# Block sums ordered between bank emptyings, and a weight sum made from another, in a two-layer hybrid attention trunk

## The chip, the cores and the metric

The kernel runs on one core of a Trainium2 chip. The core has five engines with instruction streams of their own: PE (matrix products), DVE (elementwise and reductions), ACT (pointwise functions and copies), POOL (elementwise on SBUF only) and SP (here it only issues DMAs). Each engine takes its instructions in the order in which the compiler put them, and one that waits holds up those behind it. The metric is the device time of one execution in microseconds (us), lower is better.

## The reference

A batch of one, 1024 tokens, width 1024, two layers, all in float32:

```python
for l in range(DEPTH):
    h = rmsnorm(x, norm1[l])
    proj = h @ w_in[l]
    qa, ka, va, qb, kb, vb, gate_pre = jnp.split(proj, splits, axis=-1)
    o_a = dilated_mixture(...)            # 12 heads in 3 groups of (window, dilation)
    o_b = stick_breaking_attention(...)   # 4 heads
    gates = jax.nn.sigmoid(gate_pre + b_gate[l])
    merged = g_a * (o_a @ w_br[l, :OUT_A]) + g_b * (o_b @ w_br[l, OUT_A:])
    x = x + merged @ w_o[l]
    up = rmsnorm(x, norm2[l]) @ w_up[l]
    a = causal_depthwise_conv(up[..., :D_FF], conv_w[l], conv_b[l])
    x = x + (jax.nn.gelu(a, approximate=False) * up[..., D_FF:]) @ w_down[l]
return rmsnorm(x, norm_f)
```

## The kernel before, in words

**Products.** Activations lie with features on the partitions and tokens in two halves of 512 columns. A float32 product is made of three matmuls: each operand is split into a high and a low part of a shorter type (ACT casts the high part, DVE subtracts it to get the low one; `split`, lines 138 and 145), and high x high, high x low and low x high are summed in a PSUM bank. "Emptying" a bank means reading it with ACT and DVE so that it can be used again; the tag "ps" has two banks.

**Seven products for eight.** Two 512-row halves of the contraction, two column blocks and two token halves form a 2 x 2 block product, done with seven block products instead of eight (a scheme of Strassen's kind). It needs sums of blocks on both sides. On the side of the weights `pair` (line 1055 on) makes them for each pair of column blocks: a raw tile `in_a` of four blocks a11, a12, a21, a22 is loaded, and its sums are formed on POOL (lines 1078 and 1080) and DVE (1084 and 1089), then split (`piece`) into the weights w1 to w7. On the side of the activations `block_sums` (line 1005 on) forms, once per layer and for each of four feature chunks i, from the blocks b11, b12, b21, b22 of h: sum 1 = b12 - b11, sum 3 = b22 - b12, sum 2 = b11 + sum 3 (DVE lines 1020, 1016, 1023) and sum 4 = b21 - sum 2 (POOL line 1026), and splits them (`in_two`) into S[1] to S[4]. `seven` (line 999 to 1001) issues the matmuls of one block product: 12 of them, in two steps of six.

**The stages of a layer.** First the *head*: queries, keys and values of the first two stick-breaking heads are made the plain way (`values_part`, banks v_ps, emptied on lines 576 and 577; `kq_half`, banks kq_ps and q_ps, emptied on lines 592 to 596). The block sums are issued beside it. Then the *attention*: 16 stick-breaking items (B), 4 near items (N) and 16 dilated items (T). Between their small steps the class `Dense` puts steps of the remaining projections, 18 pairs per layer, as filler: after each small step of an item, `advance(rate)` adds `rate` to what is due and runs one step (six matmuls) for each whole one. The rates are RATE by query block for B, RATE_N for N and RATE_T for T. Then come the branch projections, w_o, and the feed-forward part, which has blocks of its own and which the change doesn't touch.

**What sets the order.** PE's order is the order of the program text. The other engines' order is made by the compiler's list scheduler, in which what is emitted earlier goes first when it can; `tc.add_manual_dep(..., NO_SYNC)` adds an edge that keeps one instruction behind another in that order without a wait, SYNC one with a wait. `LAST["head"]` names the last two emptyings (ACT, DVE) of the head emitted so far, `LAST["h"]` the last instruction that makes h. A list `todo` in `block_sums` holds the small jobs; while the head runs, one job is popped after each step of the head (`dense.aside()`). `dense.prime(1)` runs one preparing step of the first pair. A pair prepares itself in six such steps (READY): load, first POOL sum or sums, w1, then w5 with the DVE sum for w6, then w6, then the DVE sum for w3. Later pairs take these steps while the pair before them runs.

**Buffers.** The raw tile `in_a` has two buffers ("ql"), the result tile `u` of a pair two ("wr", 1024 columns: halves u1 and u2). POOL writes the weight sum a11 - a21 into u2 of the new `u` (line 1078), and from there w7 is split; later u2 holds results.

**Only in the first layer**: h of the first 384 tokens is put together again from its two parts by POOL (`again`, line 1971 on, instruction 1977), eight instructions, into RAW[0, 0] (b12) and RAW[0, 1] (b22), alternating between them.

Of the kernel before, what the change touches and what calls it, by code (L numbers as in the profile page):

```python
# [7 lines left out]
F32 = mybir.dt.float32  # L8
# [4 lines left out]
ALU = mybir.AluOpType  # L13
# [3 lines left out]
P = 128  # L17
T = 1024
D = 1024
KD = D // P  # L20
HF = 512
# [11 lines left out]
NRAW = 2  # L33
# [5 lines left out]
SYNC = mybir.DependencyInfo(mybir.DependencyClass.Sync, mybir.DependencyReason.DATA)  # L39
NO_SYNC = mybir.DependencyInfo(mybir.DependencyClass.NoSync, mybir.DependencyReason.DATA)  # L40
IN_ORDER = {ET.PE, ET.Activation, ET.DVE, ET.Pool}
HEAD = 4
SECOND = 0.35
RATE = (1.1, 1.25, 1.35, 1.4)
RATE_N = 0.75
RATE_T = 0.55
EARLY = 5
LEAD = 6
LEAD_N = 7
# [7 lines left out]
def f32(ap):  # L57
    return ap.bitcast(F32)
# [3 lines left out]
def trunk_kernel(ctx, tc, x, norm1, w_in, b_gate, w_br, w_o, norm2, w_up, conv_w, conv_b, w_down, norm_f, out, depth=None, probe=None):  # L62
    nc = tc.nc
    act, dve, pe, pool = nc.scalar, nc.vector, nc.tensor, nc.gpsimd
# [4 lines left out]
    sb = ctx.enter_context(tc.tile_pool(name="sb", bufs=1))  # L69
# [15 lines left out]
    LAST = {}  # L85
# [39 lines left out]
    def small(name, dtype=F32):  # L125
        return sb.tile([P, 512], dtype, tag="pt", bufs=PT, name=name)
# [8 lines left out]
    def split(hi, lo, src, turn=None, behind=None):  # L135


        one = act.copy(hi, src)  # L138
        if behind:
            tc.add_manual_dep(one.ins, behind[0], NO_SYNC, reason="behind")  # L140
        if turn == "is":
            LAST["act"] = one.ins.name
        elif turn == "waits" and "act" in LAST:
            tc.add_manual_dep(one.ins, LAST["act"], NO_SYNC, reason="in turn")
        two = dve.tensor_tensor(lo, src, f32(hi), ALU.subtract)  # L145
        if behind:
            tc.add_manual_dep(two.ins, behind[1], NO_SYNC, reason="behind")
        if turn == "is":
            LAST["dve"] = two.ins.name
        return two  # L150
# [285 lines left out]
    H = [[None, None], [None, None]]  # L436
# [51 lines left out]
    S, B = {}, {}  # L488
# [15 lines left out]
    RAW = {}  # L504
# [479 lines left out]
    def yields(one):  # L984

        for k in ("red", "dve"):
            if k in LAST:
                tc.add_manual_dep(one.ins, LAST[k], NO_SYNC, reason="in turn")

    def piece(src, turn=None):  # L990
        hi = sb.tile([P, 512], F32R, tag="wh", bufs=4, name="w_hi")
        lo = sb.tile([P, 512], F32R, tag="wl", bufs=4, name="w_lo")
        yields(split(hi, lo, src, turn))
        return hi, lo
# [10 lines left out]
    def block_sums(dense):  # L1005


        b12, b22, b11, b21 = (lambda i, n=n, k=k: RAW[n, k][:, i, :] for n in range(2) for k in range(2))

        s3 = {}  # L1010

        def sum3(i):
            if i % 2 == 0:
                s3[i] = sb.tile([P, 2, HF], F32, tag="p4", bufs=4, name="h_sum")
                s3[i], s3[i + 1] = s3[i][:, 0, :], s3[i][:, 1, :]
            one = dve.tensor_tensor(s3[i], b22(i), b12(i), ALU.subtract)
            tc.add_manual_dep(one.ins, LAST["h"], NO_SYNC, reason="behind h")

        def sum1(i):
            dve.tensor_tensor(b12(i), b12(i), b11(i), ALU.subtract)  # L1020

        def sum2(i):
            dve.tensor_tensor(b11(i), b11(i), s3[i], ALU.add)

        def sum4(i):
            pool.tensor_tensor(b21(i), b21(i), b11(i), ALU.subtract)

        def in_two(t, i):
            if i == 0:
                if t == 4:  # L1030
                    S[4] = half(0, 0)
                else:
                    new_s(t)
            split(*S[t][i], {1: b12, 2: b11, 3: s3.get, 4: b21}[t](i), "waits", LAST["head"] if t > 2 else None)

        def front(i):
            sum3(i)
            sum1(i)
            in_two(1, i)
            sum2(i)  # L1040

        todo = [(set(), lambda i=i: front(i)) for i in range(4)]
        todo += [(set(), lambda: dense.prime(1)), (set(), lambda: [sum4(i) for i in range(4)])]
        todo += [({"wv"}, lambda: dense.prime(1))]
        todo += [(set(), lambda i=i: in_two(2, i)) for i in range(4)]
        todo += [(set(), lambda: dense.prime(1)) for _ in range(2)]

        def begin():
            for i in range(4):
                dense.at(1 + i, lambda i=i: in_two(3, i))  # L1050
                dense.at(6 + i, lambda i=i: in_two(4, i))

        return todo, begin

    def pair(dense, l, offs, tiled, put):

        def view(x, n=None):  # L1060

            return x.rearrange("p (r j) -> p r j", r=4) if tiled else x

        def grid(o):
            return o.rearrange("p (j r) -> p r j", r=4) if tiled else o

        raw = sb.tile([P, 4, 512], F32, tag="ql", bufs=2, name="in_a")
        for c in range(2):
            one = nc.sync.dma_start(
                raw[:, 2 * c : 2 * c + 2, :].rearrange("p a (k n) -> p (a k) n", n=P),  # L1070
                w_in[l][:, offs[c] : offs[c] + P].rearrange("(k p) n -> p k n", p=P),
            )
            tc.add_manual_dep(one.ins, LAST["sv"], NO_SYNC, reason="behind")
        a11, a12, a21, a22 = (raw[:, i, :] for i in range(4))
        yield
        u = sb.tile([P, T], F32, tag="wr", bufs=NRAW, name="u")
        u1, u2 = u[:, HF:T], u[:, 0:HF]
        one = pool.tensor_tensor(u2, a11, a21, ALU.subtract)  # L1078
        tc.add_manual_dep(one.ins, LAST["again"], NO_SYNC, reason="behind")
        pool.tensor_tensor(a21, a21, a22, ALU.add)  # L1080
        yield
        w1 = piece(a11)
        yield
        yields(dve.tensor_tensor(a11, a21, a11, ALU.subtract))
        w5 = piece(a21, "waits")
        yield
        w6 = piece(a11)
        yield
        yields(dve.tensor_tensor(a11, a12, a11, ALU.subtract))
        yield  # L1090
        w3 = piece(a11, "waits")
        u5 = small("u5")
        pa, pc = bank("ps", "i_a"), bank("ps", "i_c")
        yield from seven(pa, w1, half(1, 0), True, True)
        yield
        with tc.high_priority(offset=AHEAD):
            act.copy(view(u1), grid(pa))
        w7 = piece(u2, "waits")
        yield from seven(pc, w5, S[1], True, True)
        yield  # L1100
        with tc.high_priority(offset=AHEAD):
            act.copy(view(u5), grid(pc))
        w2 = piece(a12)
        yield from seven(pa, w6, S[2], False, True)
        with tc.high_priority(offset=AHEAD):
            act.copy(view(u2), grid(pa))
        w4 = piece(a22)
        dense.last(0)
        yield
        yield "turn"  # L1110
        yield from seven(pc, w3, half(0, 1), False, True)
        with tc.high_priority(offset=AHEAD):
            dve.tensor_tensor(view(u2), view(u2), grid(pc), ALU.add)
        put(0, 0, u2, False, a11)
        yield
        yield "turn"
        yield from seven(pa, w7, S[3], False, True)
        with tc.high_priority(offset=AHEAD):
            dve.tensor_tensor(view(u5), view(u5), grid(pa), ALU.add)
        put(1, 0, u5, False, a21)  # L1120
        dense.last(1)
        yield
        yield "turn"
        pb = bank("ps", "i_b")
        yield from seven(pb, w2, half(1, 1), True, True)
        with tc.high_priority(offset=AHEAD):
            dve.tensor_tensor(view(u1), view(u1), grid(pb), ALU.add)
        put(0, 1, u1, False, a12)
        yield
        yield "turn"  # L1130
        for word in seven(pa, w4, S[4], False, True):
            yield
            yield "turn"
        with tc.high_priority(offset=AHEAD):
            put(1, 1, grid(pa), True)
        yield
# [83 lines left out]
    def mixer(l, pending):  # L1220
# [44 lines left out]
        for j in range(16):  # L1265
            items.append((f"B{j}", [f"FB{j // 4 * 4 + 3}"], [], RATE[3 - j % 4], lambda j=j: stick_item(dense, j // 4, 3 - j % 4)))
        for v in range(4):
# [616 lines left out]
    def first():  # L1884
# [7 lines left out]
        wv = early["wv"] = []  # L1892
# [78 lines left out]
        def again():  # L1971

            t = slice(0, 3 * P)
            for e in range(KD):
                k = e % 2
                hi, lo = (f32(y[:, 4 * k + e // 2, t]) for y in H[0])
                one = pool.tensor_tensor(RAW[0, k][:, e // 2, t], hi, lo, ALU.add)
                tc.add_manual_dep(one.ins, LAST["h"], NO_SYNC if e else SYNC, reason="after h")
            LAST["again"] = one.ins.name

        def fill(n):
# [19 lines left out]
        f = [scaled(i) for i in range(8)]  # L2001
# [92 lines left out]
```

## Time and profile before

| what | value |
|---|---|
| device time, median of 3 runs | 2668.99 us (2664.97 to 2672.4) |
| device time of the profiled execution | 2669.75 us |
| its span, first to last instruction | 2667.6 us |
| mean granted clock of PE | 0.994 |
| busy PE / DVE / ACT / POOL, us | 2619.4 / 2072.7 / 1347.4 / 696.2 |
| head of layer 0, until its first pair | up to 77.17 us |
| head of layer 1, until its first pair | up to 1390.75 us |

The device time of the profiled execution is 2.15 us above its span. A row of a timeline reads: start in us, duration in us, engine (with q: its queue), line, operation, written tile <- read tiles, shapes, how many in a row, and in brackets how long the engine was idle before it and what ended that. A row of the waits reads: who waited for whom: us in total, times, the longest. A row of the windows reads: stretch, its length, busy time of PE, PE's weight loads, DVE, ACT and POOL with the number of instructions, PE's granted clock (1.00 is full), the share of the DMA engines and GB/s. A row of the groups ends in: busy us, mean ns of one | idle us before them.

### The profile page before, as it was taken

The numbers are of one execution on the slowest core, as the hardware profiler recorded it, in microseconds if no ns is written. First come the engines' busy times: TensorE is split into PE (matmuls) and PEld (weight loads), VectorE is DVE, ScalarE is ACT, GpSimd is POOL, SyncE is SP. The second block draws the span as 40 slices with busy tenths as digits, with TensorE's granted clock in tenths as the row PEclk, the third lists the DMA queues.
The fourth block names the chain that finished last, engine by engine and source line by source line (L and its number), as shares of the span: only waits on it lengthen the run. The fifth ranks groups of instructions, "written<-read, shape, count | busy, mean of one in ns | idle before, by whom it ended". The sixth has DMA issues, their size and how long they took to land.

```text
span 2667.6 us, 36682 instructions
## 1 busy us (share of the span) xinstructions
PE 2619.4 (98%) x12732; PEld 2190.2 (82%) x12732; DVE 2072.7 (78%) x3110; ACT 1347.4 (51%) x2500; POOL 696.2 (26%) x588
## 2 busy tenths in 40 slices
PE   8999999999999999999999999999999999999999
PEld 7887888888888888888888877888888888888887
DVE  7876767685888988897678777667858888898865
ACT  5545566564555554532445555666645455554225
POOL 4222110122233443321123112111321343344200
PEclk9999999999999999999999999999999999999999
DMA  6543487883244544688444344787732544446863
GB/s 226 154 123 107 144 216 204 201 262 107 83 139 146 171 137 156 227 317 318 151 131 147 121 133 140 207 226 194 233 99 71 175 141 151 150 168 248 339 243 116
DMA packets 400422, 468.26 MB, mean 176 GB/s; under 512 B 24308, under 2 KB 315500, under 8 KB 398444
## 3 DMA queue, kind: packets, MB, share of 16 engines
q1 hardware_dynamic: 400220, 465.90, 54.3%
q8 instruction: 101, 1.65, 0.3%
q14 instruction: 85, 0.70, 0.1%
q10 hardware_dynamic: 16, 0.00, 0.0%
HBM read 303.23 MB, written 162.59 MB: 175 GB/s over the span
## 4 chain that ended last, share of the span: by engine, by line
PE 84%; DVE 9%; DMA 3%; ACT 2%; issue 2%; POOL 0%; SPq 0%; DVEq 0%; ACTq 0%; POOLq 0%
PE u_a L999 5%; PE u_a L1000 5%; PE u_a L1001 5%; PE d_ps L1708 5%; PE d_ps L1710 4%; PE d_ps L1709 4%; PE i_a L999 4%; PE i_a L1001 4%; PE i_a L1000 4%; PE u_c L999 3%; PE u_c L1000 3%; PE u_c L1001 3%; PE o_ps L181 2%; PE o_ps L179 2%; PE o_ps L180 2%; PE i_c L999 2%
## 5 line engine op out<-in xcount | busy, mean ns | idle before, releaser
L145 DVE TENSOR_TENSOR w_lo<-up_a,w_hi 128x512 fp32r<-128x512 f32 x240 | 237.4, 996 | 21.7 <-ACT w_hi L138 21.7
L138 ACT CAST w_hi<-up_a 128x512 fp32r<-128x512 f32 x240 | 149.3, 622 | 185.4 <-PE u_a L1000 45.4
L138 ACT CAST w_hi<-in_a 128x512 fp32r<-128x512 f32 x216 | 134.1, 621 | 185.3 <-PE i_a L1000 71.3
L1716 DVE TENSOR_TENSOR x<-x,d_ps 128x512 f32<-128x512 f32 (+1 forms) x228 | 152.0, 671 | 77.9 <-PE d_ps L1710 76.7
L145 DVE TENSOR_TENSOR w_lo<-in_a,w_hi 128x512 fp32r<-128x512 f32 x216 | 161.4, 748 | 51.7 <-ACT w_hi L138 43.7
L1447 POOL TENSOR_TENSOR cv<-cv 128x512 f32<-128x512 f32 x88 | 132.3, 1515 | 249.6 <-DVE cv L1442 139.4
L1078 POOL TENSOR_TENSOR u<-in_a 128x512 f32<-128x512 f32 x36 | 52.6, 1460 | 399.9 <-DMA in_a<-in_w_in_dram 118.0
L145 DVE TENSOR_TENSOR g<-cv,g 128x512 fp32r<-128x512 f32 x154 | 152.2, 990 | 5.2 <-ACT g L138 2.7
L1708 PE MATMUL d_ps<-gd_in,w_hi 128*128 128x512 f32 (+1 forms) x340 | 130.3, 383 | 1.5 <-ACT w_hi L138 0.7
L1710 PE MATMUL d_ps<-gd_in,w_lo 128*128 128x512 f32 (+1 forms) x340 | 129.8, 382 | 0.0
L1709 PE MATMUL d_ps<-gd_in,w_hi 128*128 128x512 f32 (+1 forms) x340 | 129.8, 382 | 0.0
L999 PE MATMUL u_a<-hh,w_hi 128*128 128x512 f32 x320 | 124.7, 390 | 2.0 <-DVE u L1598 2.0
L1001 PE MATMUL u_a<-t_hi,w_lo 128*128 128x512 f32 x320 | 124.5, 389 | 0.0
L1000 PE MATMUL u_a<-hl,w_hi 128*128 128x512 f32 x320 | 124.5, 389 | 0.0
L1000 PE MATMUL u_a<-t_lo,w_hi 128*128 128x512 f32 x320 | 124.5, 389 | 0.0
L1001 PE MATMUL u_a<-hh,w_lo 128*128 128x512 f32 x320 | 124.5, 389 | 0.0
L999 PE MATMUL u_a<-t_hi,w_hi 128*128 128x512 f32 x320 | 124.5, 389 | 0.0
L720 DVE TENSOR_TENSOR_SCAN stay<-stay,zero 128x512 f32<-128x512 f32 (+2 forms) x96 | 97.2, 1020 | 33.2 <-POOL stay L707 33.0
L999 PE MATMUL i_a<-t_hi,w_hi 128*128 128x512 f32 x288 | 119.9, 416 | 0.0
L999 PE MATMUL i_a<-hh,w_hi 128*128 128x512 f32 x288 | 119.2, 414 | 0.0
L138 ACT CAST g<-cv 128x512 fp32r<-128x512 f32 x154 | 95.0, 617 | 41.4 <-POOL cv L1447 29.9
L1001 PE MATMUL i_a<-t_hi,w_lo 128*128 128x512 f32 x288 | 114.5, 398 | 0.0
(384 smaller groups left out, 8443.4 us busy)
## 6 DMA issues: line engine op xcount, KB each, us to landing
gd<-g SPq DMA_DIRECT2D x154, 512.0 KB, 3.5
gd_in<-gd SPq DMA_DIRECT2D x154, 512.0 KB, 5.7
up_a<-in_w_up_dram SPq DMA_DIRECT2D x80, 512.0 KB, 5.3
in_a<-in_w_in_dram SPq DMA_DIRECT2D x72, 512.0 KB, 5.6
wd_raw<-in_w_down_dram SPq DMA_DIRECT2D x22, 1024.0 KB, 11.4
gin<-gs SPq DMA_DIRECT2D x32, 512.0 KB, 4.6
w_raw<-in_w_o_dram SPq DMA_DIRECT2D x64, 256.0 KB, 2.8
gs<-u SPq DMA_DIRECT2D x48, 256.0 KB, 3.6
```

The lines of the kernel that those rows point to most:

```text
L138: one = act.copy(hi, src)
L145: two = dve.tensor_tensor(lo, src, f32(hi), ALU.subtract)
L179: pe.matmul(o, lh, rh, start=(first and i == 0), stop=False, skip_group_check=share)
L720: one = dve.tensor_tensor_scan(rev, rev, zero[:, 0:1].to_broadcast([P, c1 - c0]), 1.0 if c1 == L else sv[:, c1 : c1 + 1], ALU.mult, ALU.add)
L999: pe.matmul(o, w[0][:, c], rh, start=(first and i == 0), stop=False, skip_group_check=True)
L1000: pe.matmul(o, w[0][:, c], rl, start=False, stop=False, skip_group_check=True)
L1001: pe.matmul(o, w[1][:, c], rh, start=False, stop=(last and i == 3), skip_group_check=True)
L1447: return lambda: pool.tensor_tensor(dst, a, b, ALU.subtract)
L1708: pe.matmul(o[:, sub], wh[:, c], gh[:, sub], start=(i == 0 and k in (0, 4, 5)), stop=False, skip_group_check=True)
L1709: pe.matmul(o[:, sub], wh[:, c], gl[:, sub], start=False, stop=False, skip_group_check=True)
L1710: pe.matmul(o[:, sub], wl[:, c], gh[:, sub], start=False, stop=(i == m - 1), skip_group_check=True)
L1716: dve.tensor_tensor(x, x, o[:, sub], ALU.add)
```

## The change

Four things are changed.

1. In `block_sums` sum 1 comes first for all four chunks and is written to a new tile (`free`, tag "p4") instead of over b12; sum 3 and sum 2 come later, together, as `sum32`. Every one of them is now put behind the emptying of the head that was emitted last (`behind`), and so are all splits (`in_two`; before: those of S[3] and S[4] only). The list of jobs is rewritten: sum 1 and S[1] in the first four jobs, then sum 3 with sum 2 chunk by chunk, sum 4, and S[2] in two jobs with an empty one between.
2. In `pair` the POOL sum a11 - a21 is gone. In its place POOL makes a22 - w6 (the same value, as w6 = a21 + a22 - a11), into a21, in the sixth preparing step, just ahead of the DVE sum for w3 that overwrites w6. The tile `u` is taken after the preparing steps, and w7 is split from a21.
3. The filler rates of the stick-breaking items fall by 0.05 each, that of the dilated ones rises from 0.55 to 0.62.
4. In `again` the order follows b12, then b22, and each of the eight instructions is synchronised with the last part of h emitted by then (before: the first only).

```diff
-RATE = (1.1, 1.25, 1.35, 1.4)
+RATE = (1.05, 1.2, 1.3, 1.35)
...
-RATE_T = 0.55
+RATE_T = 0.62
...
+        def behind(one, eng=1):
+            tc.add_manual_dep(one.ins, LAST["head"][eng], NO_SYNC, reason="behind")
 
         def sum1(i):
-            dve.tensor_tensor(b12(i), b12(i), b11(i), ALU.subtract)
-
-        def sum2(i):
-            dve.tensor_tensor(b11(i), b11(i), s3[i], ALU.add)
+            one = dve.tensor_tensor(free(1, i), b12(i), b11(i), ALU.subtract)
+            behind(one)
+            tc.add_manual_dep(one.ins, LAST["h"], NO_SYNC, reason="behind")
+
+        def sum32(i):
+            behind(dve.tensor_tensor(free(3, i), b22(i), b12(i), ALU.subtract))
+            behind(dve.tensor_tensor(b11(i), b11(i), room[3, i], ALU.add))
...
-        def front(i):
-            sum3(i)
-            sum1(i)
-            in_two(1, i)
-            sum2(i)
-
-        todo = [(set(), lambda i=i: front(i)) for i in range(4)]
-        todo += [(set(), lambda: dense.prime(1)), (set(), lambda: [sum4(i) for i in range(4)])]
-        todo += [({"wv"}, lambda: dense.prime(1))]
-        todo += [(set(), lambda i=i: in_two(2, i)) for i in range(4)]
-        todo += [(set(), lambda: dense.prime(1)) for _ in range(2)]
...
+        todo = [
+            do(*each(sum1, (0,), (1,))),
+            do(*each(sum1, (2,), (3,))),
+            do(*each(in_two, (1, 0), (1, 1))),
+            do(*each(in_two, (1, 2), (1, 3))),
+            do(prime),
+            do(*each(sum32, (0,))),
+            do(*each(sum32, (1,))),
+            do(*each(sum32, (2,))),
+            nothing,
+            do(*each(sum32, (3,)), *each(sum4, (0,), (1,), (2,), (3,))),
+            ({"wv"}, prime),
+            do(*each(in_two, (2, 0), (2, 1))),
+            nothing,
+            do(*each(in_two, (2, 2), (2, 3))),
+            do(prime),
+            do(prime),
+        ]
...
         yield
-        u = sb.tile([P, T], F32, tag="wr", bufs=NRAW, name="u")
-        u1, u2 = u[:, HF:T], u[:, 0:HF]
-        one = pool.tensor_tensor(u2, a11, a21, ALU.subtract)
+        one = pool.tensor_tensor(a21, a21, a22, ALU.add)
         tc.add_manual_dep(one.ins, LAST["again"], NO_SYNC, reason="behind")
-        pool.tensor_tensor(a21, a21, a22, ALU.add)
         yield
         w1 = piece(a11)
...
+        pool.tensor_tensor(a21, a22, a11, ALU.subtract)
         yields(dve.tensor_tensor(a11, a12, a11, ALU.subtract))
         yield
         w3 = piece(a11, "waits")
+        u = sb.tile([P, T], F32, tag="wr", bufs=NRAW, name="u")
+        u1, u2 = u[:, HF:T], u[:, 0:HF]
         u5 = small("u5")
...
-        w7 = piece(u2, "waits")
+        w7 = piece(a21, "waits")
...
             for e in range(KD):
-                k = e % 2
-                hi, lo = (f32(y[:, 4 * k + e // 2, t]) for y in H[0])
-                one = pool.tensor_tensor(RAW[0, k][:, e // 2, t], hi, lo, ALU.add)
-                tc.add_manual_dep(one.ins, LAST["h"], NO_SYNC if e else SYNC, reason="after h")
+                hi, lo = (f32(y[:, e, t]) for y in H[0])
+                one = pool.tensor_tensor(RAW[0, e // 4][:, e % 4, t], hi, lo, ALU.add)
+                tc.add_manual_dep(one.ins, LAST["h"], SYNC, reason="after h")
```

More of the change, by code (lines that the diff above doesn't have):

```diff
@@ L1008, in block_sums, with free @@
         b12, b22, b11, b21 = (lambda i, n=n, k=k: RAW[n, k][:, i, :] for n in range(2) for k in range(2))
-        s3 = {}
-        def sum3(i):
+        room = {}
+        def free(t, i):
             if i % 2 == 0:
[L1014 to L1017, printed above, removed]
-        def sum1(i):
-            dve.tensor_tensor(b12(i), b12(i), b11(i), ALU.subtract)
-        def sum2(i):
-            dve.tensor_tensor(b11(i), b11(i), s3[i], ALU.add)
+                x = sb.tile([P, 2, HF], F32, tag="p4", bufs=4, name="h_sum")
+                room[t, i], room[t, i + 1] = x[:, 0, :], x[:, 1, :]
+            return room[t, i]
+        def behind(one, eng=1):
+            tc.add_manual_dep(one.ins, LAST["head"][eng], NO_SYNC, reason="behind")
+        def sum1(i):
+            one = dve.tensor_tensor(free(1, i), b12(i), b11(i), ALU.subtract)
[4 more added lines that the diff above has]
+            behind(dve.tensor_tensor(b11(i), b11(i), room[3, i], ALU.add))
         def sum4(i):
@@ L1033, in in_two, with do, each @@
                     new_s(t)
-            split(*S[t][i], {1: b12, 2: b11, 3: s3.get, 4: b21}[t](i), "waits", LAST["head"] if t > 2 else None)
-        def front(i):
-            sum3(i)
-            sum1(i)
-            in_two(1, i)
-            sum2(i)
-        todo = [(set(), lambda i=i: front(i)) for i in range(4)]
-        todo += [(set(), lambda: dense.prime(1)), (set(), lambda: [sum4(i) for i in range(4)])]
-        todo += [({"wv"}, lambda: dense.prime(1))]
-        todo += [(set(), lambda i=i: in_two(2, i)) for i in range(4)]
-        todo += [(set(), lambda: dense.prime(1)) for _ in range(2)]
+            src = room[t, i] if t in (1, 3) else (b11 if t == 2 else b21)(i)
+            split(*S[t][i], src, "waits", LAST["head"])
+        def do(*fs):
+            return set(), lambda: [f() for f in fs]
+        def each(f, *args):
+            return [lambda x=x: f(*x) for x in args]
+        nothing = (set(), lambda: None)
+        prime = lambda: dense.prime(1)
+        todo = [
[16 more added lines that the diff above has]
+        ]
         def begin():
```

## The prediction, made before the changed kernel was run

> **What bounds the kernel now.** The page comes first, for the engine that is nearly always busy.
>
> ```profile
> span 2667.6 us, 36682 instructions
> PE 2619.4 (98%) x12732; PEld 2190.2 (82%) x12732; DVE 2072.7 (78%) x3110; ACT 1347.4 (51%) x2500; POOL 696.2 (26%) x588
> ```
>
> PE is the bound, and the change neither adds nor removes a matmul. What can be won is 48.2 us in which PE is idle, and what its clock loses behind such waits. So the waits of PE are next, the longest first.
>
> ```profile
> PE kq_ps L179 <- DVE vb L577: 9.3, 1, 9.3
> PE sb_o L745 <- DVE vv L1181: 5.9, 2, 2.9
> PE q_ps L179 <- DVE kq_l L593: 4.3, 1, 4.3
> PE sb_t L732 <- DVE beta L724: 3.6, 2, 1.9
> PE z L636 <- DMA t_kq<-tk: 2.9, 3, 1.6
> ```
>
> These five rows are 26.0 us in nine waits. The first lies in the head of layer 0, the third in that of layer 1; sb_o and sb_t belong to stick-breaking items, z <- t_kq to dilated ones. The windows around them show what the clock adds.
>
> ```profile
> 50.00:75.00 25.00, 15.73 (x80) 13.52 (x80) 21.33 (x26) 8.27 (x15) 8.85 (x6) 0.80 0.35 115
> 250.00:275.00 25.00, 22.07 (x101) 18.05 (x100) 12.72 (x21) 11.18 (x23) 4.66 (x7) 0.86 0.31 106
> 625.00:650.00 25.00, 25.00 (x112) 20.68 (x111) 10.61 (x16) 9.50 (x16) 5.10 (x4) 1.00 0.37 107
> 1350.00:1375.00 25.00, 20.66 (x88) 16.85 (x88) 24.84 (x29) 9.39 (x18) 16.67 (x11) 0.93 0.53 163
> 1550.00:1575.00 25.00, 22.08 (x119) 18.45 (x118) 16.72 (x27) 10.84 (x20) 4.14 (x6) 1.00 0.34 105
> ```
>
> At full clock an undisturbed stretch issues 112 large matmuls in 25 us, 0.223 us each; a filler step of six is 1.34 us. The wait at 257 is followed by a lowered clock (0.86), the equally long one at 1571 is not (1.00).
>
> **The change part by part. The head of layer 0.** DVE's timeline shows what stands ahead of the emptying that PE waits for, and PE's what the wait leaves behind.
>
> ```profile
> 47.19 2.10 DVE L1016 TENSOR_TENSOR h_sum<-h_raw 128x512 f32<-128x512 f32 x2
> 62.47 0.68 DVE L1023 TENSOR_TENSOR h_raw<-h_raw,h_sum 128x512 f32<-128x512 f32 x1
> 63.07 1.27 DVE L577 TENSOR_TENSOR vb<-v_ps,vb 128x512 fp32r<-128x512 f32 x2
> 64.97 2.48 DVE L145 TENSOR_TENSOR t_lo<-h_raw,t_hi 128x512 fp32r<-128x512 f32 x4
> 71.81 0.69 DVE L596 TENSOR_TENSOR kq_l<-kq_ps,kq_h 128x512 fp32r<-128x512 f32 x1 [1.64 <-ACT kq_h L595]
> 72.42 0.68 DVE L145 TENSOR_TENSOR w_lo<-in_a,w_hi 128x512 fp32r<-128x512 f32 x1
> ```
> ```profile
> 63.80 0.80 PE L179 MATMUL kq_ps<-hh,kq_w 128*128 128x512 f32 x1 [9.27 <-DVE vb L577]
> 67.31 0.40 PE L181 MATMUL kq_ps<-hh,kq_w 128*128 128x512 f32 x1
> 70.99 0.39 PE L179 MATMUL q_ps<-hh,kq_w 128*128 128x512 f32 x1
> 76.20 0.39 PE L181 MATMUL q_ps<-hh,kq_w 128*128 128x512 f32 x1
> 77.17 0.50 PE L999 MATMUL i_a<-hh,w_hi 128*128 128x512 f32 x1
> ```
>
> PE has the values in their two banks at 63.80 - 9.27 = 54.53. From 47.19 on DVE works through four chunks of four instructions (sum 3, sum 1, low part of S[1], sum 2), 16 in the 15.88 us until 63.07, 0.99 each, and only then empties the two banks. After the wait PE is slow: from 63.80 to 67.31 lie 8 intervals, 3.51 us, where the 23 intervals from 70.99 to 76.20 take 0.2265 each, so 1.81; the price is 1.70. Wait and clock cost 10.97.
>
> After the change only eight of the 16 are emitted ahead of the first emptying (four sums 1, four low parts); sums 3 and 2 are kept behind it. At the same 0.99 these end at 47.19 + 7.9 = 55.1, the emptying (1.27 / 2 = 0.64) at 55.8. PE waits 1.3 instead of 9.27. Then keys run for 24 x 0.2265 = 5.4 until 61.2, while DVE has six sums (5.9 at 0.99, 3.7 at the 0.62 of the quiet row x4) and the second emptying: done between 60.1 and 62.3, so at most 1.1 is left, of which I take 0.5. **Gain: 10.97 - 1.3 - 0.5 = 9.2.** Bounds: 10.97 if both leftovers vanish; 2.4 in the first rival below.
>
> What is late next: the first pair, which starts at 77.17 now and at 68 then. S[1] is done by 55, and the first preparing steps stand at the same places of the head. S[2] is needed two products (24 matmuls, 5.4 us) after the start, at 73.4. In DVE's queue 29 instructions stand from 47.19 to the end of the row at 72.42 (73.10), with that row's 1.64 idle and a little more among them: 24 us of work, which, started at 47.19, ends at 71. It is enough, with 2 us to spare. The loads of the stick items' keys and of the second pair are issued behind the same emptyings and move with them.
>
> **`again`.** Three of its eight POOL instructions ran early, beside DVE; now all eight run late.
>
> ```profile
> 33.43 2.94 POOL L1977 TENSOR_TENSOR h_raw<-hh,hl 128x384 f32<-128x384 f32 x3
> 35.41 1.52 DVE L145 TENSOR_TENSOR hl<-h_raw,hh 128x512 fp32r<-128x512 f32 x1 [0.21 <-ACT hh L138]
> 42.34 5.81 POOL L1977 TENSOR_TENSOR h_raw<-hh,hl 128x384 f32<-128x384 f32 x5 [5.96 <-DVE hl L145]
> ```
>
> The DVE row beside them takes 1.52 where a quiet one takes 0.62; it may win 0.9. The eight then end at 42.34 + 8 x 1.16 = 51.6, with b12 complete at 47.0, in time for sum 1. Beside the sums DVE may lose what the three took, up to 2.9. I take 0 of -0.9 to +2.9.
>
> **The head of layer 1.** Here the emptying of the queries stands behind the sums.
>
> ```profile
> 1358.09 0.68 DVE L596 TENSOR_TENSOR kq_l<-kq_ps,kq_h 128x512 fp32r<-128x512 f32 x1
> 1358.69 1.78 DVE L1016 TENSOR_TENSOR h_sum<-h_raw 128x512 f32<-128x512 f32 x2
> 1370.77 0.68 DVE L593 SCALAR_TENSOR_TENSOR kq_l<-q_ps,kq_h 128x512 fp32r<-128x512 f32 x1
> 1371.50 0.80 PE L179 MATMUL q_ps<-hh,kq_w 128*128 128x512 f32 x1 [4.34 <-DVE kq_l L593]
> ```
>
> PE finished the matmuls before at 1367.16. Twelve sums fill the 12.1 us from 1358.69 to 1370.77. Four of them, or eight with the low parts, are ahead of the queries' emptying after the change: 4 to 8 us at 1.0, done at 1363.4 to 1367.4, about when PE comes. The wait of 4.34 goes, and with it the low clock (0.93), for which I take layer 0's 1.70. **Gain: 6.0**, between 4 and 6.
>
> **The pair's sums, and u late.** One of the two waits of sb_o:
>
> ```profile
> 252.19 1.77 POOL L1078 TENSOR_TENSOR u<-in_a 128x512 f32<-128x512 f32 x1 [5.89 <-PE v_t L1175]
> 253.09 0.59 ACT L704 ACTIVATE stay<-z 128x512 f32<-128x512 f32 x1
> 255.53 0.30 POOL L707 TENSOR_SCALAR_AFFINE_SELECT stay<-stay 128x128 f32<-128x128 f32 x1
> 255.86 1.23 DVE L720 TENSOR_TENSOR_SCAN stay<-stay,zero 128x512 f32<-128x512 f32 x1 [3.05 <-POOL stay L707]
> 259.15 0.55 PE L745 MATMUL sb_o<-sbh,kv 128*128 128x256 f32 x1 [2.93 <-DVE vv L1181]
> ```
>
> POOL stands 5.89 us for a free `u`, which the transposes of a value pair still read; then two weight sums run, and the selects of the stick item, behind them, hold up DVE's scan and with it the emptying that PE wants. After the change POOL needs no `u`, and its first sum is done while it now idles. What is late next is ACT's row, done at 253.68: two selects of 0.3 end at 254.3, not 255.83. So 1.5 us of each wait go for sure, and all 2.93 if DVE's order changes too; the clock (0.86 of 25 us, 3.5 us missing, some of it on the wait itself) is worth about 2 in layer 0. Both layers: 2 x 1.5 + 2 = 5 to 2 x 2.93 + 2 = 7.9. **I take 6.** The waits of sb_t come the same way; ahead of one of them a weight sum stands between the two selects:
>
> ```profile
> 1403.51 1.29 POOL L1078 TENSOR_TENSOR u<-in_a 128x512 f32<-128x512 f32 x1
> 1404.76 0.29 POOL L707 TENSOR_SCALAR_AFFINE_SELECT stay<-stay 128x128 f32<-128x128 f32 x1
> ```
>
> That sum's 1.29 goes; of the 3.6 I take **1.5**, between 0 and 3.6.
>
> The sum is not free. It moves to the last preparing step, and the DVE sum that overwrites w6 must now wait for it, with DVE's queue behind it: scans, low parts, emptyings.
>
> ```profile
> L1080 POOL TENSOR_TENSOR in_a<-in_a 128x512 f32<-128x512 f32 x36 | 53.6, 1488 | 2.5
> L1084 DVE TENSOR_TENSOR in_a<-in_a 128x512 f32<-128x512 f32 x36 | 24.5, 682 | 0.4
> ```
>
> Nearest row: the DVE sum L1084 also reads what POOL made, two steps earlier, and DVE idles 0.4 us ahead of all 36. Upper bound: each of the 36 waits a whole POOL sum and PE with it, 36 x 1.488 = 53.6. Nothing speaks for a gain. The compiler can put other DVE work between, and w3 is wanted six steps (8 us) later; I stay near the row and take **a loss of 2**.
>
> **The rates.** Per group of four stick items the filler falls from 36.7 steps to 35.3 (10, 8, 6 and 4 advances by their rates), 5.6 per layer; 16 dilated items with five advances each get 16 x 5 x 0.07 = 5.6 more. No work goes, 7.5 us of it move. The dilated stage has the waits z <- t_kq (2.9), which more filler could shorten; the stick stage has less cover. I take 0, between -3 and +15 (third rival).
>
> **Sum**: 9.2 + 0 + 6.0 + 6 + 1.5 - 2 + 0 = 20.7. The profiled execution took 2669.75 (span and 2.15 around it), 0.76 above the median of the runs shown. From the median: 2668.99 - 20.7 = **2648.3**.
>
> **Two rules of the skill.** The Trainium skill, "TensorE: Matmul & The Clock Gate", Part 1, lets the clock fall only after a whole idle window of about 3.4 us. The trace disagrees: 2.93 us brought 0.86. By the rule the leftover of 1.3 us in layer 0 would cost no clock, as in the sum. The Trainium skill, "SBUF — State Buffer", "Who interferes with whom", says that a DVE instruction with two SBUF inputs contends with POOL reading SBUF. The rows 1.52 against 0.62 agree; it is why `again` is in the first rival.
>
> **The rivals.**
>
> 1. *DVE stays the bound of the first head.* POOL's late instructions and the moved sums slow DVE as they do now: 29 instructions at 0.99 end at 75.9, 2.5 after S[2] is wanted, and both waits bring the low clock, 2 x 1.70. For: 0.99 against 0.62. Against: POOL is done at 51.6, not throughout. Layer 0 then gains 9.2 - 2.5 - 3.4 = 3.3, less up to 0.9 of `again`, so 2.4 at the least; time 2655.
> 2. *It doesn't do what it says.* "Behind" only orders; if the compiler puts all six further sums ahead of the emptying in layer 0, 14 x 0.99 + 0.64 end at 61.7, and only 2.1 of 9.27 goes, the clock not: 2655.5.
> 3. *Filler is missed in the stick stage.* If all 7.5 us per layer turn into waits there while the dilated stage gets no shorter, 15 are lost: 2663. Against: the waits found in that stage have a POOL sum or ACT ahead, not missing filler.
> 4. *Slower.* The DVE sum waits for the whole POOL sum. 147 of a layer's 252 filler steps lie in stick items, 10.5 pairs, 21 in both layers: 21 x 1.488 = 31. It outweighs the 22.7 of the other terms from 16 pairs on: 2677. Against: L1084's 0.4.
>
> **How the numbers follow.** Forecast (2642 to 2654) 0.57; more than that, with all of sb_o, sb_t and the second emptying (about 2639) 0.11; rivals 1 and 2 together 0.14; rival 3 0.10; rival 4 0.08. A measurement of this kernel can tell 0.3%, 8 us, from no change. Faster by more: the first three cases, 0.82, less 0.02 for their upper edge, 0.80; within: rival 3 and that edge, 0.12; slower: 0.08. The range 2638 to 2662 leaves out rival 4, half of rival 3 and the best tail.
>
> **What would show it.** In the new profile kq_ps <- vb should be under 2 us, q_ps <- kq_l gone, the first pair start near 68 and the windows at 50 and 1350 show 0.95 or more; sb_o <- vv under 3 in total, with POOL's first sum no longer ended by v_t. Wrong would be: a wait of i_a on t_lo near 73; DVE idle ahead of the sum for w3, released by POOL, with several microseconds in total; new waits of sb_o or sb_t on parts, where filler ran out.

## The result, and the profile after

The changed kernel takes 2648.67 us (median of 4 runs, 2646.70 to 2652.54) against 2668.72 before: a ratio of 0.9927, 95% interval 0.9909 to 0.9945. The forecast was 2648.3. The sum came out; its terms did not, and most of what follows is about that. The profiled execution took 2646.70, with a span of 2644.8.

The page of the kernel after, busy time by engine:

```profile
span 2644.8 us, 36724 instructions
PE 2614.3 (99%) x12732; PEld 2183.7 (83%) x12732; DVE 2064.3 (78%) x3110; ACT 1345.3 (51%) x2500; POOL 691.4 (26%) x588
```

PE's idle time fell from 48.2 to 30.5 us, 17.7 of the 22.8 by which the span is shorter; the other 5 are busy time of matmuls, fewer of which run at a low clock (mean granted clock 0.998 for 0.994). PE's waits after, in the columns explained above:

```profile
PE v_ps L179 <- DVE kq_l L596: 3.8, 1, 3.8
PE kq_ps L179 <- DVE vb L577: 2.6, 1, 2.6
...
PE v_t L1196 <- DVE vv L1202: 2.2, 4, 1.1
...
PE i_a L999 <- DVE kq_l L596: 1.3, 1, 1.3
...
PE sb_o L745 <- DVE vv L1202: 0.6, 2, 0.3
...
PE sb_t L732 <- DVE beta L724: 0.3, 1, 0.3
```

In the attention most is gone: sb_o 5.9 to 0.6, sb_t 3.6 to 0.3, and z <- t_kq isn't in the list; v_t rises from 0.3 to 2.2. In the heads it is not: kq_ps <- vb still waits, and two waits are new, both on kq_l, the emptying of a bank of keys. The windows of the kernel after:

```profile
50.00:75.00 25.00, 20.84 (x101) 16.92 (x100) 24.90 (x34) 10.64 (x20) 13.20 (x9) 0.93 0.34 114
250.00:275.00 25.00, 24.91 (x128) 20.74 (x128) 18.23 (x31) 14.86 (x31) 3.04 (x7) 1.00 0.48 170
1350.00:1375.00 25.00, 21.19 (x128) 19.29 (x127) 19.39 (x25) 8.27 (x15) 8.66 (x6) 0.93 0.35 117
```

The head of each layer (at 50 and 1350) still loses clock and PE time; the stretch at 250 is full.

**The same by stage.** Stages that hold more or fewer filler steps can't be compared by length. So take from PE's timeline, for every interval between the starts of two matmuls, what it is longer than 0.437 ns for each column of the first (at least 0.055 us), and add it up. This *excess* holds waits, low clock and pipeline losses, and leaves out the matmuls themselves. The heads run from the first v_ps to the first i_a, the attention from there to the first br_ps, both layers together, and elsewhere counts from the first v_ps on; before has 29.7 us of excess in the heads, 120.4 in the attention, 40.8 elsewhere. Against that, for all kernels of this study:

| kernel (parts of the change) | ratio to before, 95% interval | heads | attention | elsewhere |
|---|---|---|---|---|
| the change (1 to 4) | 0.9927 (0.9909 to 0.9945) | -5.5 | -17.2 | 0.0 |
| e1: 1 | 0.9957 (0.9942 to 0.9972) | -10.6 | -0.7 | +0.1 |
| e2: 1, 4 | 0.9968 (0.9956 to 0.9980) | -9.5 | -1.3 | +1.2 |
| e3: 2 | 0.9979 (0.9969 to 0.9988) | -2.5 | -4.8 | -2.1 |
| e4: 3 | 0.9947 (0.9930 to 0.9963) | 0.0 | -14.9 | +0.7 |
| e5: 1, 3 | 0.9898 (0.9883 to 0.9912) | -10.5 | -15.7 | +0.6 |
| e6: 1, 2, 3 | 0.9911 (0.9897 to 0.9926) | -5.3 | -14.1 | +0.7 |
| e7: 1, 2, 3, emptyings first | 0.9897 (0.9880 to 0.9913) | -11.7 | -15.3 | +0.1 |
| e8: 2 with u early | 1.0000 (0.9991 to 1.0010) | -1.5 | +1.9 | -1.5 |
| e9: 3, dilated rate only | 0.9996 (0.9987 to 1.0006) | -1.0 | +0.8 | -1.7 |
| e10: 3, stick rates only | 0.9931 (0.9915 to 0.9948) | +2.1 | -16.5 | -3.4 |
| e11: 1, 3, emptyings first | 0.9910 (0.9896 to 0.9925) | -11.1 | -14.6 | +0.2 |
| e12: as e11, double shift | 0.9922 (0.9907 to 0.9937) | -9.7 | -8.1 | -2.4 |

The ratios are of all executions; the columns are of the one that was profiled, which lay 3.5 us under the median in e3 and 2.9 over it in e6, so columns of different kernels compare to a few us only.

Of the change's 22.7 us the heads gave 5.5 and the attention 17.2. The forecast had 15.2 and 5.5. The attention's excess can be split further: PE's waits (idle for more than 0.15 us) are 16.8 before, 5.7 after and 7.4 in e10; what other intervals lose at half clock is 6.9, 0 and 0; the rest stays, 96.6, 97.4 and 96.4. So the gain there is waits and the low clock behind them, and nothing else.

**Where the first head's gain went.** DVE in the head of layer 0, after; then POOL beside it:

```profile
46.95 5.77 DVE L1022 TENSOR_TENSOR h_sum<-h_raw 128x512 f32<-128x512 f32 x4
52.64 3.56 DVE L145 TENSOR_TENSOR t_lo<-h_sum,t_hi 128x512 fp32r<-128x512 f32 x4
56.12 0.68 DVE L577 TENSOR_TENSOR vb<-v_ps,vb 128x512 fp32r<-128x512 f32 x1
...
71.41 0.68 DVE L596 TENSOR_TENSOR kq_l<-kq_ps,kq_h 128x512 fp32r<-128x512 f32 x1
```
```profile
42.07 10.10 POOL L1997 TENSOR_TENSOR h_raw<-hh,hl 128x384 f32<-128x384 f32 x8 [8.02 <-DVE hl L145]
```

The order is the one forecast: four sums, four low parts, the emptying. But a sum takes 1.44 us (5.77 / 4), not 0.99, while POOL's eight instructions run until 52.17. PE waits 2.60, and here that costs the clock (0.93). Then the keys' second bank is emptied only at 71.41, behind the pair's sums, and the first pair, which needs that bank, starts at 72.15 instead of 68.

**Where the second head's went.** ACT and DVE of layer 1, after:

```profile
1359.06 0.62 ACT L138 CAST w_hi<-in_a 128x512 fp32r<-128x512 f32 x1 [7.16 <-DVE in_a L1108]
1359.58 2.17 ACT L138 CAST t_hi<-h_sum 128x512 fp32r<-128x512 f32 x4
1361.66 0.57 ACT L595 CAST kq_h<-kq_ps 128x512 fp32r<-128x512 f32 x1
```
```profile
1357.25 1.77 DVE L1108 TENSOR_TENSOR in_a<-in_a 128x512 f32<-128x512 f32 x1
...
1362.27 0.69 DVE L596 TENSOR_TENSOR kq_l<-kq_ps,kq_h 128x512 fp32r<-128x512 f32 x1 [1.87 <-ACT kq_h L595]
```

The queries' emptying is in time, as forecast, and q_ps <- kq_l is gone. The next in line, the emptying of the second bank of keys (kq_h, kq_l), stands in ACT's queue behind the cast of w3, which waits for the DVE sum of line 1108, and behind four parts of S[1]. PE waits 3.81 us for that bank in place of 4.34 for the other.

### The profile page after: what moved, and what is told of

Its sections match the earlier page's. It is cut to its first block, busy times and chain, and to the rows that moved or that the text cites. A ratio compares the mean times of both kernels' runs of the same rounds, so it can differ in the third digit from the quotient of the medians.

```text
span 2644.8 us, 36724 instructions
## 1 busy us (share of the span) xinstructions
PE 2614.3 (99%) x12732; PEld 2183.7 (83%) x12732; DVE 2064.3 (78%) x3110; ACT 1345.3 (51%) x2500; POOL 691.4 (26%) x588
## 5 line engine op out<-in xcount | busy, mean ns | idle before, releaser
L138 ACT CAST w_hi<-in_a 128x512 fp32r<-128x512 f32 x252 | 156.2, 621 | 182.4 <-PE i_a L1000 50.3
L145 DVE TENSOR_TENSOR w_lo<-in_a,w_hi 128x512 fp32r<-128x512 f32 x252 | 184.8, 735 | 58.5 <-ACT w_hi L138 52.2
L1107 POOL TENSOR_TENSOR in_a<-in_a 128x512 f32<-128x512 f32 x36 | 52.9, 1470 | 260.0 <-issue 123.2
L1097 POOL TENSOR_TENSOR in_a<-in_a 128x512 f32<-128x512 f32 x36 | 50.0, 1388 | 252.8 <-DMA in_a<-in_w_in_dram 142.2
```

What stands on the lines that cost most here:

```text
L1107: pool.tensor_tensor(a21, a22, a11, ALU.subtract)
```

## The experiments

Theories: **A**, the forecast's split (sums 15.2, pair 5.5, rates 0). **B**, the split read from the two traces: the heads give about 5, and most of the attention's gain is due to the rates. Twelve kernels follow.

**e1 and e2: the sums alone, and with `again`.** e1 is before with the diff's `block_sums`; e2 adds the diff's `again`. What e2 has over e1:

```diff
-                k = e % 2
-                hi, lo = (f32(y[:, 4 * k + e // 2, t]) for y in H[0])
...
-                tc.add_manual_dep(one.ins, LAST["h"], NO_SYNC if e else SYNC, reason="after h")
+                hi, lo = (f32(y[:, e, t]) for y in H[0])
...
+                tc.add_manual_dep(one.ins, LAST["h"], SYNC, reason="after h")
```

> Part 1 alone (the block sums and their jobs; POOL's putting h together, the pair and the rates as before). As forecast, the sums give 15.2 us: 2654. Read from the two traces, the heads gave only 5.5 in all (first pair of layer 0 at 72.15 for 77.17; layer 1's head 52.4 long for 52.9): 2663. If the late POOL instructions of part 4 are what slowed the first four sums (5.77 us for 3.97 by the forecast's 0.99 each), the wait kq_ps <- vb is about 1 here and the first pair starts near 70, some 7 us gained in layer 0; the attention stages keep before's waits (sb_o, sb_t, z on t_kq).

> Parts 1 and 4 (sums, and POOL's eight instructions all late). As forecast, the same as part 1 alone. If POOL's late instructions slow the sums, this is 2 to 4 us slower than part 1 alone: kq_ps <- vb 2.6 us with the low clock behind it, first pair at about 72, as in the changed kernel; total 2663.

Measured: e1 2657.77, e2 2658.89, the intervals of their ratios overlapping. The first four sums, in e1 and then in e2:

```profile
47.23 4.40 DVE L1022 TENSOR_TENSOR h_sum<-h_raw 128x512 f32<-128x512 f32 x4
```
```profile
45.86 5.79 DVE L1022 TENSOR_TENSOR h_sum<-h_raw 128x512 f32<-128x512 f32 x4
```

So `again` does slow the four sums, 1.10 to 1.45 us each. PE's waits in e1:

```profile
PE sb_o L745 <- DVE vv L1202: 5.9, 2, 2.9
...
PE i_a L999 <- DVE kq_l L596: 2.3, 1, 2.3
...
PE v_ps L179 <- DVE kq_l L596: 1.6, 1, 1.6
...
PE kq_ps L179 <- DVE vb L577: 1.2, 1, 1.2
```

kq_ps <- vb is the 1.3 of the forecast (1.2), and the clock stays full in the window from 50 to 75; with `again` it is 3.6 and that window has 0.93. The first pair then comes 1.1 us later in the head of e2, not 2 to 4, for e1 has a longer wait at i_a. Alone the sums give the heads 10.6, not 15.2 (A) nor the 5.5 of the full change (B): another part takes 4 to 5 of it away. e5 and e6 show which.

**e3: the pair alone.** Against before:

```diff
-        u = sb.tile([P, T], F32, tag="wr", bufs=NRAW, name="u")
-        u1, u2 = u[:, HF:T], u[:, 0:HF]
-        one = pool.tensor_tensor(u2, a11, a21, ALU.subtract)
+        one = pool.tensor_tensor(a21, a21, a22, ALU.add)
...
+        pool.tensor_tensor(a21, a22, a11, ALU.subtract)
...
+        u = sb.tile([P, T], F32, tag="wr", bufs=NRAW, name="u")
+        u1, u2 = u[:, HF:T], u[:, 0:HF]
...
-        w7 = piece(u2, "waits")
+        w7 = piece(a21, "waits")
```

> Part 2 alone (w7 from w6 and u late). As forecast 5.5: 2663.5, all of it in the stick items: sb_o <- vv gone, sb_t less. Read from the two traces, the stick stages gave 17.4 us in length, of which the rates only moved some 15 to the dilated stage; waits and clock there fell by 6.7. So 2662, with the dilated stage's loss (23.05 and 22.35 us over the issue pace) as before. If the wait of POOL for u is the cause, no wait of sb_o on vv over 1 us is left, with the rates still the old ones.

Measured 2663.65, a gain of 5.0 where the forecast had 5.5. PE's waits in e3:

```profile
PE v_t L1175 <- DVE vv L1181: 4.2, 5, 2.4
...
PE sb_o L745 <- DVE vv L1181: 2.3, 2, 1.2
```

sb_o fell from 5.9 to 2.3, not below 1 each: what is next late is DVE's and ACT's part of the chain, as the forecast worked it out, and part of the wait went to the transposes (v_t).

**e4, e9 and e10: the rates, and each half.**

```diff
-RATE = (1.1, 1.25, 1.35, 1.4)
+RATE = (1.05, 1.2, 1.3, 1.35)   # e4 and e10
-RATE_T = 0.55
+RATE_T = 0.62                   # e4 and e9
```

> Part 3 alone (filler moved from stick to dilated items). As forecast 0: 2669. Read from the two traces, the dilated stages lost 8.5 us less over the issue pace and the near ones 2.0, and no wait of z on t_kq is left; if the rates are the cause of that, 2659 to 2661, with before's waits of sb_o and sb_t still there. The third rival: 2684, waits in the stick items in place of the moved steps.

> Only the dilated rate (0.62), the stick rates as before. If the dilated stage's own shortage of filler is what part 3 cures, its waits of z on t_kq and the clock behind them go (some 6 us) and the stick stage keeps sb_o <- vv at 5.9: 2662. If it is the stick stage that gains, by filler and items meeting elsewhere, this is near 2669.

> Only the stick rates (0.05 less each), the dilated rate as before. If the stick stage's meeting of POOL's wait for u with a stick item is moved by it, sb_o <- vv falls under 1 and 6 to 7 us go: 2662. By the third rival of the forecast filler is missed in the stick items: more waits there, 2669 or more. The two halves should add up to the 13.8 of part 3.

Measured: e4 2654.83, a gain of 13.8 where A had none; e9 2668.45, no difference that can be told; e10 2651.83, a gain of 17.9. So the rates were the largest part of the change, and all of it comes from taking filler out of the stick items; more filler in the dilated ones gives nothing. B was right about the rates and wrong about the place. The two halves make 19.1 against 13.8 for e4; the intervals don't tell that difference.

PE's waits in e9 keep the stick stage's, and have new ones at the join of the two mixers; then in e10, where sb_o is down to 0.6 and z <- t_kq is gone too:

```profile
PE sb_o L745 <- DVE vv L1181: 5.9, 2, 2.9
PE sb_t L732 <- DVE beta L724: 4.6, 3, 1.6
...
PE j_ps L970 <- DVE ot L652: 4.1, 2, 2.1
```
```profile
PE sb_t L732 <- DVE beta L724: 1.6, 1, 1.6
...
PE sb_o L745 <- DVE vv L1181: 0.6, 2, 0.3
```

POOL of e10 around the former wait of sb_o:

```profile
254.72 1.29 POOL L1078 TENSOR_TENSOR u<-in_a 128x512 f32<-128x512 f32 x1 [6.29 <-PE v_t L1175]
256.09 1.30 POOL L1080 TENSOR_TENSOR in_a<-in_a 128x512 f32<-128x512 f32 x1
261.26 0.29 POOL L707 TENSOR_SCALAR_AFFINE_SELECT beta<-beta 128x128 f32<-128x128 f32 x1 [3.87 <-ACT beta L703]
```

POOL still stands for the transposes of the value pair, 6.29 us, and both weight sums still follow. But the next stick item's selects come 3.87 us after them, not right behind them as at 252 before. The wait was a *meeting* of a preparing step with a stick item's selects, and a shift of 4% in the rate undoes the meeting in both layers (in layer 1 of e10 the sums end at 1564.54 and the selects start at 1568.41).

**e5: sums and rates without the pair.** It is e1 with the rates of e4.

> Parts 1 and 3, without the pair's new sum and without the late POOL instructions. If the singles add (10.9 and 13.8), 2644: the change's other parts cost 4.7 together, because with the rates shifted no wait is left that the pair's new sum removes, and in the heads that sum delays the emptyings (layer 1: v_ps <- kq_l 3.8 us in the changed kernel, 1.6 with the sums alone). If instead the pair's part is needed, 2650 or more, with sb_o <- vv back near 5.9.

Measured 2645.05, ratio 0.9898: the singles add up, and the pair's part isn't needed. Compared by ratio, the change without parts 2 and 4 is 0.3% faster than the change, but the two intervals overlap at their ends, so this is not settled. In the heads e5 gains 10.5, the full change 5.5: the 5 us are what parts 2 and 4 cost there. It is part 2, for e6, the change without part 4, gains no more there (5.3), and part 4 alone costs 1.1 between e1 and e2.

**e6: the change without `again`.** It is the changed kernel with the diff shown for e2 taken back.

> The changed kernel without part 4 (POOL's eight instructions as before). The runs of parts 1 and of 1 with 4 differ by 1.1 us in the profiled spans: 2647.5 by that. If POOL's late work is what slows the first four sums, kq_ps <- vb falls from 2.6 to about 1.2 and the low clock behind it goes; up to 3 us: 2645.5. By the forecast's step (0): 2648.7.

Measured 2647.72, the same as the change. Its longest waits:

```profile
PE v_ps L179 <- DVE kq_l L596: 3.8, 1, 3.8
PE i_a L999 <- DVE kq_l L596: 3.5, 1, 3.5
```

The wait kq_ps <- vb left the list of the longer waits, but i_a <- kq_l rose from 1.3 to 3.5 and v_ps <- kq_l stayed 3.8: the time that the faster sums win is lost again at the next bank. The forecast's 0 for `again` holds for the total.

**e7 and e11: the emptyings first.** Both have the emptyings of the head's banks in a block of high priority; e7 is e6 with it, e11 is e5 with it.

```diff
+            with tc.high_priority(offset=AHEAD):
                 one = act.copy(vv[:, :, :, 0:64], ov)
                 two = dve.tensor_tensor(vv[:, :, :, 64:128], ov, ...)
...
+        with tc.high_priority(offset=AHEAD):
             LAST["head"] = in_parts(c, SCALE, hi, lo, o)
```

> As the run without part 4, and the emptyings of the head's banks get priority over all else on ACT and DVE in the compiler's list. If the queue's order is what is left of the waits in the heads (v_ps <- kq_l 3.8, i_a <- kq_l 1.3, kq_ps <- vb 1.2 to 2.6 and the clock behind them), they all fall under 1 and the time by 4 to 8 us: 2638 to 2643. If the data (sums on DVE, too much work for the stretch) is the bound, the waits come back at the first pair (i_a or i_c on t_lo or w_lo): 2645 to 2648.

> Parts 1 and 3 with the head's emptyings first in the list: without the pair's new sum and without the late POOL instructions. If the two gains add (3.6 less than the changed kernel without the pair's part, some 4 less by the emptyings first), 2640 to 2642; if the emptyings first only repaired what the pair's sum had delayed, 2644 to 2645.

Measured: e7 2643.64, 4.1 us under e6 (the intervals of the ratios overlap; in the heads of the profiled executions it gains 11.7 for 5.3), with these waits left in the heads:

```profile
PE i_a L1001 <- DVE kq_l L597: 2.0, 1, 2.0
PE v_ps L179 <- DVE kq_l L597: 1.8, 1, 1.8
```

e11 2646.17, no better than e5. So it fits that the pair's new sum had spoilt the order of the queues: priority repairs that, and in a head without that sum it finds next to nothing to repair (11.1 for 10.5 in the heads). The banks still wait about 2 us each: not all of it is order. e7 and e5 have the lowest ratios (0.9897 and 0.9898); they are not told apart from each other, nor from e11.

**e8: u taken early.** e3, but the POOL sum goes into u2 of a `u` taken in the sixth preparing step.

```diff
-        pool.tensor_tensor(a21, a22, a11, ALU.subtract)
+        u = sb.tile([P, T], F32, tag="wr", bufs=NRAW, name="u")
+        u1, u2 = u[:, HF:T], u[:, 0:HF]
+        pool.tensor_tensor(u2, a22, a11, ALU.subtract)
...
-        w7 = piece(a21, "waits")
+        w7 = piece(u2, "waits")
```

> Part 2 alone, but the sum a22 - w6 goes into u as before, which is taken in the sixth preparing step: POOL still waits for a free u, though two sums no longer follow each other. If the wait for u is the cause, sb_o <- vv stays near 5.9 and the gain of 5.0 is lost: 2668. If it was the block of two sums, 2664 as with part 2 alone.

Measured 2671.09: the gain of 5.0 is lost, as expected if the wait for `u` counts, but not where that says. PE's waits in e8:

```profile
PE i_a L999 <- DVE u L1127: 4.5, 2, 3.1
...
PE sb_o L745 <- DVE vv L1181: 2.4, 2, 1.3
```

sb_o is as short as in e3, so it was splitting the block of two sums that cut it, not the late `u`. The loss stands elsewhere, in i_a <- u, where a stick item's select came behind a weight sum that waited for its load: another meeting. The ratios of e3 and e8 do differ by more than their intervals; whether the late `u` is worth that by itself, or only by where this meeting falls, stays open.

**e12: twice the shift.** e11 with the shift doubled:

```diff
-RATE = (1.05, 1.2, 1.3, 1.35)
+RATE = (1.0, 1.15, 1.25, 1.3)
...
-RATE_T = 0.62
+RATE_T = 0.69
```

> As the run beside it, with twice the shift of filler (stick rates 0.1 under before's, dilated 0.69). If the gain of part 3 comes from the amount of filler in the dilated items, some more goes: 2 to 5 us under the run beside it. If it came from where filler and items happen to meet, this is as likely slower, by a wait like sb_o's of 3 us and the clock behind it; if the stick items run short, by up to 15 us.

Measured 2648.72, 2.5 us over e11 (the intervals overlap), with waits of the old kind back:

```profile
PE sb_t L734 <- DVE beta L726: 3.1, 3, 2.0
PE sb_o L747 <- DVE vv L1204: 2.7, 2, 1.4
...
PE j_ps L972 <- DVE ot L654: 2.1, 2, 1.1
```

More of the same shift is not better, which fits meetings and not an amount of filler.

## Why the prediction was right in its total and wrong in its terms

- **The head of layer 0 (9.2).** Wrong in size: the full change gives 5.0 there (77.17 to 72.15); parts 1 and 4 alone give 6.0 and part 1 alone 7.1, by the head's length from its first v_ps. The mechanism held: eight instructions ahead of the emptying instead of sixteen. Two steps failed. The pace of 0.99 was taken from a stretch in which POOL worked part of the time; beside POOL's eight instructions the sums ran at 1.44, as the first rival has it, so the leftover wait was 2.60 for 1.3, and the clock was lost. And "what is late next" was looked for in S[2], where the trace after shows no wait; the late one was the second emptying of keys, 1.32 us ahead of the first pair.
- **The head of layer 1 (6.0).** Wrong: 0.5. The step that failed asked only whether the emptying that PE waits for is moved forward. It was; the bank after it was not, in ACT's queue behind w3's cast, and took its place with 3.81 us. Without the pair's new sum that wait is 1.6 and the head gains 3.5.
- **`again` (0).** Right for the total (e6), but not because it is free: DVE's first four sums are 1.4 us slower together (e1, e2), and in the changed kernel the next bank's wait hides that.
- **The pair's sums (6 and 1.5, less 2).** Right in total: part 2 alone gives 5.0. DVE's idle time ahead of the sum for w3 is 4.5 us over 36, 3.7 of it for POOL, in this row of the kernel after:

```profile
L1108 DVE TENSOR_TENSOR in_a<-in_a 128x512 f32<-128x512 f32 x36 | 25.6, 710 | 4.5 <-POOL in_a L1107 3.7
```

  So rival 4 fell, and the nearest row was the right one to stay near. Of the two reasons given for the gain, no wait for `u` and a sum out of the selects' way, e8 leaves the second for sb_o: it takes `u` early and still has 2.4. What was missed is the place where it hurts: in the heads, by the order of the queues. And with the rates shifted there is little left for it to gain; the parts overlap, so the gains of e2, e3 and e4 (9.8, 5.0, 13.8) make 28.6 and the change 20.
- **The rates (0, between -3 and +15).** The largest error, and of the wrong sign in its range: 13.8 gained. The step reasoned from the amount of filler ("the stick stage has less cover"), and e9 shows that the amount in the dilated stage is worth nothing. It did not ask which instructions of filler and item meet on POOL. The waits that go in e4 are the ones which the forecast had booked under the pair's sums (sb_o, sb_t) and, beside them, z <- t_kq.
- **The rivals.** The third, the only one about the rates, went the other way; the second did not happen, as the emptying stood where the edge put it.

The total was right by luck: heads 9.7 us too good and an attention 11.7 us too poor cancel. The check list would have said so from one profile: of its signs for the heads only q_ps <- kq_l gone came; the others (kq_ps <- vb under 2, first pair near 68, windows at 0.95) did not.

What stays open: why z <- t_kq goes with either half of the rates, and whether the waits of sb_t and z <- t_kq were meetings too; on POOL only those of sb_o were followed. Of e10's 16.5 in the attention 9.4 are waits and 6.9 the low clock behind them.

## What to carry to other kernels

When a wait on a bank is removed by reordering, list every later bank of the same rotation and find its emptying in each queue that it passes, ACT's as well as DVE's; the next one takes the wait over. When filler runs between items, a small change of its rate is a change of which instructions meet on an in-order engine: price it by the meetings in the trace, not by the amount of work moved. And run each part of a change alone, for a total that comes out as forecast proves none of its terms.

## What the runs showed of the hardware

*The clock of PE.* In these traces it falls to half in stretches of 3.41, 6.83 or 10.24 us, and a 512-column matmul then takes 0.427 us from start to start instead of 0.2265. In each trace the starts of these stretches lie whole multiples of 3.413 us apart (in before 56.98, 258.36 and 476.82, which is 59 and 64 steps). So cut the time into cells of that grid, and add up how long PE idles in each, by the ends that the profile models. In the fourteen traces, without their first 20 and last 12 us, all 28 cells at full clock with 2.0 us of idle time or more were followed by one at half clock. Of the 44 with 1.37 to 1.90 eight were, and none with less. What counts is thus the idle time within one cell and not the length of the wait. The two equal waits of sb_o before show it: the one at 256 put 2.14 us into one cell and cost the clock, the one at 1571 put 1.81 and 1.12 into two and did not. The 2.60 of the changed kernel's first head lay in one cell whole. The wait of 2.33 us at i_a cost the clock in e5, all of it in one cell, and not in e1, with 1.76 in one. So what a shorter wait saves in clock is in part chance. By the Trainium skill, "TensorE: Matmul & The Clock Gate", Part 1, it takes a whole idle window of about 3.4 us. These traces differ: 2.0 us within such a cell was always enough.

*DVE beside POOL.* The Trainium skill, "SBUF — State Buffer", "Who interferes with whom", has DVE instructions with two SBUF inputs contend with POOL reading SBUF. The traces agree: four such sums took 5.79 us in e2, where POOL's eight instructions ran beside them until 51.09, and 4.40 in e1, where POOL's five ended at 48.19 and one weight sum (1.82 us) and the start of a second fell beside them.
